# A decoder layer in split fp32 on one core: memory pairs split a block earlier, and DMA turns divided by halves of the tokens

## The chip, the cores and the metric

The kernel runs on one core of one Trainium2 chip. The metric is the device time of one execution in microseconds (us). The engines appear under short names: PE (TensorE, the matmuls; PEld is its loading of weights), ACT (ScalarE), DVE (VectorE), POOL (GpSimd) and SP (SyncE, which here issues nearly all DMAs; SPq in the profile is its DMA queue). L399 is line 399 of the kernel. A "half-word" is one of the two 16-bit halves of a 4-byte float.

## The reference

One decoder layer on 256 tokens of width 2048 with 256 memory tokens, all in float32:

```python
hn = rmsnorm(h, norm_mix_w)
q, k, v, g_ret, xr, yr, g_a, g_b = split(hn @ w_in)          # w_in: 2048 x 14336
ret_out = silu(g_ret) * head_groupnorm(retention(rotary(q), rotary(k), v))   # 8 heads
rnn_out = gelu(yr) * rg_lru(causal_dwconv(xr))
merged = sigmoid(g_a) * (ret_out @ w_proj_ret) + sigmoid(g_b) * (rnn_out @ w_proj_rnn)
h = h + merged @ w_mix_out                                   # "mix-out"
h = h + cross_attention(rmsnorm(h), rmsnorm(mem), xa_w_q, xa_w_k, xa_w_v, xa_w_o)  # 4 heads of 512
up = causal_dwconv(rmsnorm(h) @ ffn_w_up)                    # 2048 x 11264
gate, val = split(up)
h = h + (silu(gate) * val) @ ffn_w_down                      # 5632 x 2048
return rmsnorm(h, final_norm_w)
```

The work is in the matrix products with weights; each weight is read once.

## The kernel before

**Products.** Every float32 operand is split into a high part that the matmul's format holds exactly (fp32r) and the low rest, and a product is three matmuls: high by high, high by low and low by high. The weights lie in one array in the order in which they are used. A "chunk" is four tiles of 128 rows by 512 columns (1 MB). SP loads it into one of three `raw` buffers (L252); ACT copies each half of it into `hi` (L279, the cast) and DVE subtracts to get `lo` (L280). Two chunks are prepared ahead (`AHEAD`), and three chunks' worth of `hi` and `lo` are held. A chunk is 24 matmuls with 512 columns (L214). One product with 2048 rows of weights and 512 columns (a "block") is four chunks.

**Order.** PE's matmuls keep the order in which the program states them (`mm`, L213). On the other engines, SP among them, a scheduler orders the instructions; `tc.high_priority` lets what stands in it go ahead of other ready work. Work that follows a block isn't stated at once but by `later(n, fn)` (L286): `fn` is called n + 1 chunks on, so that PE has other matmuls in front of those that need its result. The same queue carries the splits, sums of squares and softmax steps.

**Turns.** A product's result has tokens on the partitions, while the next product wants features there. `by_dma` (L380) turns 256 tokens by 512 features: ACT copies the float rows into `planes` (`pl`), which holds for each half of the tokens (`tt`, 128 tokens) all low half-words and then all high ones (L388, two copies of 1024 elements per partition); SP issues two DMA transposes, one for each half of the tokens, into `turned_` (`pt`, L390); and `later(wait, join)` has ACT put the half-words together again in `f` (L399, two copies, each writing every second half-word). There are 59 turns, so 118 plane copies, 118 transposes and 118 join copies. Callers: `turned_rows` (L404: DVE first scales or copies the two halves of the rows, L412) for the rotary inputs, the convolutions' inputs, keys and queries, and the up blocks of the FFN; `two_heads` in the retention (scaling on ACT, L666); the gated merge; `residual` (L843, the sum with the residual rows `nat` is L855); and the softmax. What follows a join splits its result into the high and low operands `s` of the next products (`split_cols`, L454 on ACT and L455 on DVE, in four steps of 128x256 for a turn's two pairs) or runs the convolutions (L778, L780, L969, L971).

**Memory pairs.** The memory tokens come in already turned. `ms = Pairs(mem_t, p_mem, 3)` (L841) holds eight pairs of 128-feature tiles. `ms.load(n)` issues loads of 256 KB into `xt` (ten buffers, shared with other small tiles); asking for `ms[i]` loads three pairs further and splits pair i with `split_cols`. Pairs 0 to 3 are asked for by `memory_steps` (L877), which `residual` calls at each of the four blocks b of mix-out; the rest by the first key product itself, half-way through each of its chunks. The mix-out blocks run from about 819 to 906 us of the span, the first key block follows, and from 928 us the first query block; the last block of xa_w_o ends near 1290 us, and the first FFN block begins with what its turn yields.

The lines of memory_steps before the change:

```python
        if b == 3:
            ms.load(2)
            for k2 in range(4):
                later(k2, lambda k2=k2: ms[k2])
```

Of the kernel before, what the change touches and what calls it, by code (L numbers as in the profile page):

```python
# [12 lines left out]
U16 = mybir.dt.uint16  # L13
# [4 lines left out]
P = 128  # L18
# [18 lines left out]
FREE = 300  # L37
# [101 lines left out]
def hybrid_layer(  # L139
# [16 lines left out]
    act, dve, pe, pool, sp = nc.scalar, nc.vector, nc.tensor, nc.gpsimd, nc.sync  # L156
# [15 lines left out]
    def big(shape, dt=F32, s="b"):  # L172
        return bp.tile(shape, dt, tag="big", name=nm(s))
# [114 lines left out]
    def later(n, fn):  # L288

        pending.append((step[0] + n + 1, fn))  # L290
# [89 lines left out]
    def by_dma(rows, then, wait=1):  # L380


        planes = big([P, 2, 2, BW], U16, s="pl")
        turned_ = big([P, 2, 4, S], U16, s="pt")
        words = rows.bitcast(U16).rearrange("p t (n h) -> p h t n", h=2)
        with tc.high_priority(FREE):
            for h in range(2):
                act.copy(planes[:, :, h, :], words[:, h])  # L388
        for tt in range(2):
            sp.dma_start_transpose(  # L390
                out=turned_.rearrange("p h f s -> p (h f) s")[:, :, tt * P : (tt + 1) * P],
                in_=planes[:, tt].rearrange("p h n -> p (h n)"),
            )

        def join():
            f = big([P, 4, S], s="f")
            halves_ = f.bitcast(U16).rearrange("p f (s h) -> p h f s", h=2)
            for h in range(2):
                act.copy(halves_[:, h], turned_[:, h])  # L399
            then(f)  # L400

        later(wait, join)

    def turned_rows(a, r, then, wait=1):  # L404

        rows = big([P, 2, BW], s="rows")
        with tc.high_priority(FREE):
            for tt in range(2):
                if r is None:
                    dve.tensor_copy(rows[:, tt, :], a[:, tt, :])  # L410
                else:
                    dve.tensor_scalar_mul(rows[:, tt, :], a[:, tt, :], r[:, tt : tt + 1])  # L412
        by_dma(rows, then, wait)
# [78 lines left out]
    def sum_squares(rows, ss, c, pin=False):  # L492

        for tt in range(2):
            junk = tp.tile([P, BW], F32, tag="tmp", name=nm("junk"))
            i = act.activation(junk, rows[:, tt, :], AF.Square, accum_out=ss[:, tt, c : c + 1])
            if pin:
                tc.keep_in_program_order(i)

    def sums():  # L500
        return sp_.tile([P, 2, 4], F32, tag="ss0", name=nm("ss"))

    def rstd_rows(ss):

        var = sp_.tile([P, 2], F32, tag="var", name=nm("var"))
        dve.tensor_reduce(out=var, in_=ss, axis=AX.X, op=ALU.add)
        return rsqrt_small(var, 2, 1.0 / D, EPS)
# [97 lines left out]
    ret, words = [], []  # L605
# [5 lines left out]
    def retain(g, qr, kr, vs, dec, gates):  # L611
# [36 lines left out]
        def normalise():  # L648
            rstd = rsqrt_small(stats[:, :, 1], 8, 1.0, GN_EPS).rearrange("p (h t) -> p h t", t=2)
            for tt in range(2):  # L650
                dve.tensor_scalar_mul(rstd[:, :, tt], rstd[:, :, tt], rs0[:, tt : tt + 1])
            for hh in range(4):
                for tt in range(2):
                    y = raws[hh][:, tt, :]
                    dve.scalar_tensor_tensor(
                        out=y, in0=y, scalar=stats[:, 2 * hh + tt, 0:1],
                        in1=gates[hh // 2][:, tt, (hh % 2) * DV : (hh % 2 + 1) * DV],
                        op0=ALU.subtract, op1=ALU.mult,
                    )

            def two_heads(i):
                rows = big([P, 2, BW], s="rows")
                for hh in (2 * i, 2 * i + 1):
                    for tt in range(2):
                        c = (hh % 2) * DV
                        act.mul(rows[:, tt, c : c + DV], raws[hh][:, tt, :], rstd[:, hh, tt : tt + 1])  # L666
                by_dma(rows, words.append, 4)

            for i in range(2):
                later(i, lambda i=i: two_heads(i))  # L670
# [4 lines left out]
    for g in range(2):  # L675
# [20 lines left out]
        for b in range(2):  # L696
            a = gemm_n("w_in", 0, xs, NT, O_G + g * 1024 + b * BW)
            t = big([P, 2, BW], s="gate")
# [134 lines left out]
    for b in range(4):  # L833
        m = gated(O_GA, "w_proj_ret", ret, b, big([P, 2, BW], s="m"))
        dve.tensor_add(m, m, mb[b])
        by_dma(m, turn_merged, 1 if b < 3 else 3)
# [4 lines left out]
    ms = Pairs(mem_t, p_mem, 3)  # L841
# [35 lines left out]
    def memory_steps(b):  # L877
        if b == 0:
            ss = sums()
            for c in range(4):  # L880
                later(c, lambda c=c: sum_squares(mnat[c], ss, c))
            later(4, lambda: rsms.append(rstd_rows(ss)))
        if b == 3:
            ms.load(2)
            for k2 in range(4):
                later(k2, lambda k2=k2: ms[k2])

    h1s = []
    ss1 = residual("w_mix_out", merged, h1s, p_xa, memory_steps)


# [170 lines left out]
    for kind, b, *n in ff_plan():  # L1062
# [6 lines left out]
        else:  # L1069
            final = b + n[0] == NF // 4  # L1070
            if final:
                wfin = []
                for i in range(2):
                    t = big([P, 2, BW], s="wf")
# [39 lines left out]
```

## Time and profile before

| what | value |
|---|---|
| median of 3 runs | 2010.22 us (2009.7 to 2010.87) |
| profiled execution, its own time | 2008.91 us |
| profiled execution, span from first to last instruction | 2007.1 us |
| mean granted clock of PE | 0.999 of full speed |
| PE busy | 1995.5 us of the span |
| DVE, ACT busy | 1264.2 us, 1248.7 us |
| moved by DMA | 423.02 MB, 211 GB/s on average |

How the views are read. A row of the page's groups has line, engine, operation, output <- input with partitions x elements and type, and the number of instructions; then the busy time of all, the mean duration of one in ns, and the idle time of the engine just before them with what ended most of it. A row of the waits has the waiting engine, operation and line, what it waited for, and then the total in us, the number of times and the longest. A row of the timeline has the start and the busy time in us of a run of like instructions (x4: four of them), and in brackets how long the engine stood before and for what. Rows of DMA issues have the line, the queue, the number, the shortest, median and longest time of the issuing instruction in ns and the times of the first and last one; the row below gives the time from issue to landing. Busy times of PE overlap by its pipeline: a matmul of 0.39 us may follow the last after 0.23.

### The profile page before, as it was taken

How to read it: one execution, taken by the hardware profiler on the slowest of the kernel's cores; microseconds unless marked ns; L12 is line 12 of the kernel's file. 1: busy time of each engine (PE TensorE's matmuls, PEld its weight loads, DVE VectorE, ACT ScalarE, POOL GpSimd, SP SyncE). 2: the span in 40 equal slices, each digit the busy share in tenths (PEclk: the TensorE clock that was granted, in tenths of full speed). 3: DMA queues.
4: the chain of work that ended last, by engine and by line, in shares of the span. 5: the costliest groups of instructions: out<-in, count | busy, mean ns of one | idle time of the engine just before them, and what ended most of it. 6: DMA issues, size and time to landing. Idle time of an engine off the chain costs nothing.

```text
span 2007.1 us, 23602 instructions
## 1 busy us (share of the span) xinstructions
PE 1995.5 (99%) x9044; PEld 1661.7 (83%) x9044; DVE 1264.2 (63%) x1563; ACT 1248.7 (62%) x1506; POOL 7.7 (0%) x12
## 2 busy tenths in 40 slices
PE   9999999999999999999999999999999999999998
PEld 8888888888888888887888888888888888888887
DVE  6857757888545555457555555666775576664675
ACT  6546648888444455577666655767763566744763
POOL 0000000000000000000000000000000000000000
PEclk9999999999999999999999999999999999999999
DMA  8655657665555566787666545666565566655663
GB/s 318 237 209 168 237 201 197 225 203 186 218 197 191 192 209 212 255 255 249 198 221 213 180 170 195 222 197 232 195 226 210 199 196 219 224 209 201 209 231 126
DMA packets 189376, 423.02 MB, mean 211 GB/s; under 512 B 131664, under 2 KB 136400, under 8 KB 144208
## 3 DMA queue, kind: packets, MB, share of 16 engines
q1 hardware_dynamic: 188832, 421.00, 61.9%
q8 instruction: 70, 1.15, 0.2%
q10 hardware_dynamic: 432, 0.53, 0.1%
q14 instruction: 42, 0.34, 0.0%
HBM read 388.46 MB, written 2.10 MB: 195 GB/s over the span
## 4 chain that ended last, share of the span: by engine, by line
PE 97%; DMA 1%; issue 1%; DVE 0%; ACT 0%; SPq 0%; POOLq 0%; POOL 0%; DVEq 0%; ACTq 0%
PE acc L214 95%; PE sm L214 3%; DMA raw<-in_wall 0%; DMA pt<-pl 0%; DVE lo L280 0%; SPq L252 0%; DVE s L455 0%; SPq L533 0%; ACT f L399 0%; ACT nat L1048 0%; ACT junk L873 0%; DVE nat L855 0%; ACT pl L388 0%; ACT hi L279 0%; POOLq L1110 0%
## 5 line engine op out<-in xcount | busy, mean ns | idle before, releaser
L214 PE MATMUL acc<-hi,s 128*128 128x512 f32 (+1 forms) x5680 | 1739.0, 388 | 1.6 <-DVE s L455 1.6
L280 DVE TENSOR_TENSOR lo<-raw,hi 128x1024 fp32r<-128x1024 f32 (+1 forms) x714 | 860.2, 1219 | 645.5 <-ACT hi L279 628.6
L214 PEld LDWEIGHTS acc<-hi,s 128*128 128x128 f32 x5680 | 1061.7, 188 | 218.9 <-DVE s L455 2.4
L214 PE MATMUL acc<-lo,s 128*128 128x512 f32 (+1 forms) x2840 | 1099.8, 387 | 0.0
L279 ACT CAST hi<-raw 128x1024 fp32r<-128x1024 f32 (+1 forms) x712 | 733.7, 1048 | 500.2 <-PE acc L214 433.7
L214 PEld LDWEIGHTS acc<-lo,s 128*128 128x128 f32 x2840 | 533.2, 188 | 109.1
L399 ACT COPY f<-pt 128x1024 uint16<-128x1024 uint16 x118 | 151.5, 1348 | 76.4 <-DMA pt<-pl 76.4
L388 ACT COPY pl<-rows 128x1024 uint16<-128x1024 uint16 x90 | 89.7, 1044 | 63.8 <-DVE rows L412 55.9
L412 DVE TENSOR_SCALAR rows<-acc,ro 128x512 f32<-128x512 f32 x68 | 47.7, 742 | 3.2 <-PE acc L214 3.2
L971 DVE SCALAR_TENSOR_TENSOR fv<-f,pf,fv 128x255 f32<-128x255 f32 (+1 forms) x88 | 35.8, 477 | 0.7 <-ACT fv L969 0.7
L971 DVE SCALAR_TENSOR_TENSOR fg<-f,pf,fg 128x255 f32<-128x255 f32 (+1 forms) x88 | 35.6, 477 | 0.0
L455 DVE SCALAR_TENSOR_TENSOR s<-f,pb,s 128x256 fp32r<-128x256 f32 x48 | 20.1, 479 | 4.7 <-ACT s L454 4.7
L969 ACT ACTIVATE fv<-f,pf 128x256 f32<-128x256 f32 x44 | 22.8, 590 | 0.0
L969 ACT ACTIVATE fg<-f,pf 128x256 f32<-128x256 f32 x44 | 22.8, 591 | 0.0
L431 ACT ACTIVATE s<-fo 128x512 fp32r<-128x512 f32 x22 | 13.6, 633 | 14.2 <-DVE fo L991 14.2
L780 DVE SCALAR_TENSOR_TENSOR xr<-f,pa,xr 128x255 f32<-128x255 f32 (+2 forms) x48 | 19.9, 478 | 3.2 <-ACT xr L778 3.2
L388 ACT COPY pl<-nat 128x1024 uint16<-128x1024 uint16 x16 | 15.9, 1042 | 8.6 <-DVE nat L855 8.6
L454 ACT ACTIVATE s<-f,pb 128x256 fp32r<-128x256 f32 x48 | 20.6, 498 | 0.0
L214 PEld LDWEIGHTS sm<-s,s 128*128 128x128 f32 x144 | 18.8, 191 | 0.9
L214 PE MATMUL sm<-s,s 128*128 128x256 f32 (+1 forms) x144 | 18.6, 279 | 0.0
L214 PE MATMUL acc<-s,hi 128*128 128x512 f32 x64 | 16.5, 394 | 0.6 <-ACT hi L279 0.4
L443 ACT ACTIVATE v<-acc,ro 128x512 fp32r<-128x512 f32 x16 | 10.9, 684 | 7.7 <-DVE v L444 7.7
(152 smaller groups left out, 623.3 us busy)
## 6 DMA issues: line engine op xcount, KB each, us to landing
raw<-in_wall SPq DMA_DIRECT2D x352, 1024.0 KB, 4.9
nat<-in_x SPq DMA_DIRECT2D x8, 512.0 KB, 8.8
raw<-in_wall SPq DMA_DIRECT2D x6, 512.0 KB, 8.3
nat<-in_mem SPq DMA_DIRECT2D x4, 512.0 KB, 9.3
xt<-in_mem_t SPq DMA_DIRECT2D x8, 256.0 KB, 4.6
pt<-pl SPq DMA_TRANSPOSE x118, 4.3
xt<-in_x_t SPq DMA_DIRECT2D x7, 256.0 KB, 8.4
out<-nat SPq DMA_DIRECT2D x6, 256.0 KB, 2.8
```

The lines of the kernel that those rows point to most:

```text
L214: tc.keep_in_program_order(pe.matmul(*a, **k))
L279: act.copy(hi[:, ds], raw[:, cs, :])
L280: dve.tensor_tensor(out=lo[:, ds], in0=raw[:, cs, :], in1=hi[:, ds].bitcast(F32), op=ALU.subtract)
L388: act.copy(planes[:, :, h, :], words[:, h])
L399: act.copy(halves_[:, h], turned_[:, h])
L412: dve.tensor_scalar_mul(rows[:, tt, :], a[:, tt, :], r[:, tt : tt + 1])
L431: act.mul(t[:, :, 0:S], src, scale)
L454: act.activation(t[:, j, 0:S], src[:, j, :], AF.Identity, scale=wcol(j))
L455: dve.scalar_tensor_tensor(out=t[:, j, S:BW], in0=src[:, j, :], scalar=wcol(j), in1=t[:, j, 0:S].bitcast(F32), op0=ALU.mult, op1=ALU.subtract,
L780: dve.scalar_tensor_tensor(out=y[:, s:S], in0=z[:, 0 : S - s], scalar=p_cw(3 - s, t), in1=y[:, s:S], op0=ALU.mult, op1=ALU.add,)
L969: act.activation(y, z[:, j, :], AF.Identity, scale=pf[:, 2, t : t + 1], bias=pf[:, 3, t : t + 1])
L971: dve.scalar_tensor_tensor(out=y[:, s:S], in0=z[:, j, 0 : S - s], scalar=pf[:, 2 - s, t : t + 1], in1=y[:, s:S], op0=ALU.mult, op1=ALU.add,)
```

## The change

It has three parts. In `by_dma` the plane copies are divided by halves of the tokens instead of by halves of the words, and each half's transpose is stated right behind its copy. In `join` the two copies are divided by halves of the tokens too: each takes both half-words of 128 tokens for four tiles of features. In `memory_steps` the four memory pairs are loaded at block 2 of mix-out instead of block 3, and asked for 2 to 5 steps behind its beginning instead of 0 to 3 steps behind that of block 3, which is two chunks sooner.

```diff
@@ by_dma
-        words = rows.bitcast(U16).rearrange("p t (n h) -> p h t n", h=2)
-        with tc.high_priority(FREE):
-            for h in range(2):
-                act.copy(planes[:, :, h, :], words[:, h])
+        words = rows.bitcast(U16).rearrange("p t (n h) -> p t h n", h=2)
         for tt in range(2):
+            with tc.high_priority(FREE):
+                act.copy(planes[:, tt], words[:, tt])
             sp.dma_start_transpose(
                 out=turned_.rearrange("p h f s -> p (h f) s")[:, :, tt * P : (tt + 1) * P],
                 in_=planes[:, tt].rearrange("p h n -> p (h n)"),
@@ join
-            for h in range(2):
-                act.copy(halves_[:, h], turned_[:, h])
+            for tt in range(2):
+                cs = slice(tt * P, (tt + 1) * P)
+                act.copy(halves_[:, :, :, cs], turned_[:, :, :, cs])
             then(f)
@@ memory_steps
-        if b == 3:
+        if b == 2:
             ms.load(2)
             for k2 in range(4):
-                later(k2, lambda k2=k2: ms[k2])
+                later(2 + k2, lambda k2=k2: ms[k2])
```

The numbers of instructions on every engine stay the same, and so does the order on PE and POOL.

## Prediction

> **What bounds the kernel now.** I read the page's first part, then busy time by stretches, then what PE waited for.
>
> ```profile
> span 2007.1 us, 23602 instructions
> PE 1995.5 (99%) x9044; PEld 1661.7 (83%) x9044; DVE 1264.2 (63%) x1563; ACT 1248.7 (62%) x1506; POOL 7.7 (0%) x12
> ...
> L399 ACT COPY f<-pt 128x1024 uint16<-128x1024 uint16 x118 | 151.5, 1348 | 76.4 <-DMA pt<-pl 76.4
> L388 ACT COPY pl<-rows 128x1024 uint16<-128x1024 uint16 x90 | 89.7, 1044 | 63.8 <-DVE rows L412 55.9
> ```
>
> PE is busy for 99% of the span; ACT and DVE, where the change works, for 62% and 63%. The windows view of PE (busy time, count, granted clock, DMA share, GB/s) shows where PE has no gap at all:
>
> ```profile
> 20.00:900.00 880.00, 880.00 (x3960) 1.00 0.62 214
> 925.00:1290.00 365.00, 365.00 (x1702) 1.00 0.62 200
> 1300.00:1985.00 685.00, 685.00 (x3036) 1.00 0.62 209
> ```
>
> 1930.00 us of the three stretches are all busy at the full granted clock: nothing can be won there, only lost. What is left is the head, the tail and two places in between. PE's waits, all of them:
>
> ```profile
> PE acc L214 <- DVE s L455: 1.6, 2, 1.3
> PE warm L211 <- DVE mhalf L206: 1.1, 1, 1.1
> PE acc L214 <- DVE lo L280: 0.5, 2, 0.4
> PE acc L214 <- ACT hi L279: 0.4, 1, 0.4
> PE acc L214 <- DVE hi L277: 0.2, 1, 0.2
> ```
>
> Only the first row is made by what the diff touches: split pairs (L454/L455). The others are the warm-up and the splitting of weights at the two ends. The timeline of PE has the row's two waits, the first at a memory pair, the second at the last block of xa_w_o:
>
> ```profile
> 917.31 0.50 PE L214 MATMUL acc<-hi,s 128*128 128x512 f32 x1
> 919.08 0.50 PE L214 MATMUL acc<-hi,s 128*128 128x512 f32 x1 [1.27 <-DVE s L455]
> ...
> 1295.56 0.39 PE L214 MATMUL acc<-lo,s 128*128 128x512 f32 x1
> 1295.79 0.39 PE L214 MATMUL acc<-hi,s 128*128 128x512 f32 x1
> 1296.55 0.50 PE L214 MATMUL acc<-hi,s 128*128 128x512 f32 x1 [0.37 <-DVE s L455]
> ```
>
> Undisturbed matmuls start 0.23 us apart (1295.56 to 1295.79). From 917.31 to 919.08 are 1.77 us, so 1.54 are lost; 1295.79 to 1296.55 loses 0.53. A smaller loss of the same kind just ahead of 917.31 (0.11, by the same spacing; its rows are left out) makes 2.18 us in all, 0.11% of the time. That is the whole purse.
>
> **Step 1: memory pairs 0 to 3 loaded one block earlier and split two chunk-steps earlier.** It moves four loads of xt on SP, eight ACT and eight DVE instructions; none is added. How the stall comes about, from the timelines of ACT and DVE:
>
> ```profile
> 903.61 1.70 ACT L454 ACTIVATE s<-xt,pb 128x256 fp32r<-128x256 f32 x4
> ...
> 914.86 1.99 ACT L279 CAST hi<-raw 128x1024 fp32r<-128x1024 f32 x2
> 916.75 1.70 ACT L454 ACTIVATE s<-xt,pb 128x256 fp32r<-128x256 f32 x4
> ...
> 910.48 1.21 DVE L855 TENSOR_TENSOR nat<-nat,acc 128x1024 f32<-128x1024 f32 x1
> 918.55 1.67 DVE L455 SCALAR_TENSOR_TENSOR s<-xt,pb,s 128x256 fp32r<-128x256 f32 x4
> ```
>
> The splits of pairs 4 and 5 stand on ACT behind two casts (914.86 + 1.99) and begin at 916.75; DVE's part begins at 918.55 and PE goes on at 919.08. The changed program has these splits ahead of the casts: ACT begins them at 914.86 at the latest, 1.89 us sooner. DVE follows by about one step (1.67 / 4 = 0.42) plus its start, so the first pair is ready near 916.2 and the second near 917.2. PE wants the first at 917.31 + 0.23 = 917.54. The margin is about 1.3 us, against 1.54 missing: **the 917 loss goes, −1.65 with the small one**. Further room: the splits of pairs 0 to 3 (two rows like that at 903.61 on ACT, 3.4 us; two of 1.67 on DVE) leave this stretch for the mix-out block before, so that the sum at 910.48 can be up to 3 us sooner; I don't count it. Late next are the casts, which end 1.70 later than now (918.55 instead of 916.85). Their halves are first used a chunk-step on (24 matmuls x 0.227 = 5.4 us), so PE doesn't see it. The four loads now stand earlier on SP's queue, 256 KB each against a weight load's 1024, 1 MB in all: one weight load's work among 352, brought forward. The casts' waits for weights tell the reserve:
>
> ```profile
> ACT hi L279 <- DMA raw<-in_wall: 20.3, 14, 3.1
> ```
>
> 14 of 712 casts ever waited for a load, and PE at mid-kernel for none. Cost 0; at best also 0, since no wait of PE for a load is there to go, and at worst 3.1, the longest such wait, if the reserve were gone.
>
> **Step 2: planes by halves of the tokens.** Both ways two copies of 128x1024, each reading every second 16-bit half and writing two runs of 512; only which runs changes. Price 1.044 each as now; bounds: 0.85 (two of the 128x256 splits above at 0.425, half as many elements) and the join's 1.348. The first transpose needs only the first copy, and so is issued one copy (1.0 us) sooner; the second keeps its time or loses it to what now stands between. In the changed order, of 59 turns 29 keep their place among the weight loads, in 21 the load that stood ahead of the pair stands between its halves, in 9 behind both. What a load ahead does to a pair, from the SP issues by line (count, duration of the issue, times, and time to landing), first one pair with nothing ahead, then the pair of 1283.7, then the load ahead of that:
>
> ```profile
> L390 SPq DMA_TRANSPOSE pt<-pl x2: 1238/1286/1334, 1028.0 to 1029.3; - x2
> DMA to landing us min/median/max: 3.1/3.2/3.2
> ...
> L390 SPq DMA_TRANSPOSE pt<-pl x2: 1238/2726/4214, 1283.7 to 1285.0; - x2
> DMA to landing us min/median/max: 6.3/6.5/6.7
> ...
> L252 SPq DMA_DIRECT2D raw<-in_wall x1: 327/327/327, 1282.8 to 1282.8; - x1
> DMA to landing us min/median/max: 6.7/6.7/6.7
> ```
>
> With nothing ahead 3.2 us, behind a load 6.5. So the first half gains up to 1.0 + 3.3, the second about nothing.
>
> **Step 3: joins by halves of the tokens.** Each copy still moves 1024 elements, but as eight runs of 128 instead of one of 1024. Nearest row 1.348 (the same copy); bounds 1.044 (a plane copy) and 8 x 0.425 = 3.4, as if each run cost one of the 128x256 instructions above (1.70 / 4). I take 1.35. At the ends 118 copies would be 36 us less or 242 more of ACT's time, which has some 760 idle, 76.4 of it straight ahead of these copies. The first copy can now run while the second half travels.
>
> **The 1296 stall.** Its chain on ACT, and the DVE row that ends it:
>
> ```profile
> 1281.68 2.00 ACT L388 COPY pl<-nat 128x1024 uint16<-128x1024 uint16 x2 [1.18 <-DVE nat L855]
> 1291.38 2.56 ACT L399 COPY f<-pt 128x1024 uint16<-128x1024 uint16 x2 [1.32 <-DMA pt<-pl]
> 1294.75 1.70 ACT L454 ACTIVATE s<-f,pb 128x256 fp32r<-128x256 f32 x4
> ...
> 1296.02 1.67 DVE L455 SCALAR_TENSOR_TENSOR s<-f,pb,s 128x256 fp32r<-128x256 f32 x4
> ```
>
> Here the load falls between the halves. It waits on SP for the first transpose, now issued at 1282.7, whose issue lasts 1.24: the load goes at about 1283.95, 1.14 later than now. The second transpose follows at 1284.3, and lands, behind the load, 6.3 to 6.7 later: 1290.6 to 1291.0, or as late as 1292.4 if the load's delay of 1.14 is passed on whole to the 1291.3 of now. One copy of 1.35 then ends the join at 1292.0 to 1293.8, against 1293.94: gain 0.1 to 1.9, of which 0.53 is wanted. **I take 0.45 of the 0.53.** The delayed load feeds a chunk that PE wants about two chunk-steps of 5.4 us later, so its 1.14 costs 0.
>
> **Elsewhere.** The cover that could go is thinnest where convolutions crowd ACT and DVE:
>
> ```profile
> 313.70 2.56 ACT L399 COPY f<-pt 128x1024 uint16<-128x1024 uint16 x2 [2.62 <-DMA pt<-pl]
> 316.12 1.04 ACT L279 CAST hi<-raw 128x1024 fp32r<-128x1024 f32 x1
> 317.06 2.08 ACT L778 ACTIVATE xr<-f,pa 128x256 f32<-128x256 f32 x4
> ...
> 318.33 4.82 DVE L780 SCALAR_TENSOR_TENSOR xr<-f,pa,xr 128x255 f32<-128x255 f32 x12
> 323.06 1.22 DVE L280 TENSOR_TENSOR lo<-raw,hi 128x1024 fp32r<-128x1024 f32 x1
> ...
> 327.10 0.39 PE L214 MATMUL acc<-lo,s 128*128 128x512 f32 x1
> ```
>
> In the changed order the cast of 316.12 stands behind the convolutions and the copies after them (2.08, 1.70 and 1.99), so it ends about 5.5 later, near 322.6, its subtraction (1.22) near 323.9, for a first use at 327.10: 3.2 us are left of 8.7. So 0 here too, and up to 1.6 us of a loss only at the far end of step 3's price (two copies, 2.0 each above my value, less those 3.2, and about as much again from the next half). **Sum: −1.65 −0.45 = −2.1 us.** The profiled execution's own time is 2008.91, 1.31 under the median of 2010.22; the same difference from the median gives 2008.1.
>
> **A page weighed.** By the issue rows above the half behind a load lands with that load. The Trainium skill, "DMA: Bandwidth & Descriptors", section "Queues, rings and completion order", says that each SDMA engine consumes the descriptors of a ring in order; the trace agrees with its 3.2 us free and 6.5 us behind a load. By it alone splitting the pair around a load would bring the end of a turn nothing, and the sum would be −1.65, not −2.1.
>
> **The rivals.** *Second half no sooner.* The turn ends when the last half lands; if the load between is passed on whole (1292.4 + 1.35 = 1293.8), the 1296 stall stays and only 917 is won: 2010.22 − 1.65 = 2008.6. For it: 21 of 59 turns have a load there. Against: half of the join is already done by then. *Dearer joins.* At 3.4 a copy the last join at 1296 ends 2.05 later than I say, the stall there grows by 0.9 to 1.3, and with 917 won it is 2009.3 to 2009.8. For it: strided output; against: a copy with the same strides takes 1.348, and only the run length changes. *A new small stall* (the 323 stretch, or a moved load) eats the purse: about 2010.0, no change at all. *Slower:* in 30 turns the weight load now waits on SP behind a transpose, which itself waits for its plane copy.
>
> ```profile
> L390 SPq DMA_TRANSPOSE pt<-pl x118: 1232/1321/5372, 77.1 to 1940.3; - x118
> ```
>
> It decides once a load comes later than its reserve, two chunk-steps of 5.4 us less the 1.2 + 1.0 of cast and subtraction: some 8.6. The longest issue seen is 5.37; two such (10.7) pass it by 2.1, and PE loses 2.1 in each such turn. With three of them (6.3 less the 2.1 won) the kernel is measurably slower, with a third of the 21 turns (7) it is 15 − 2 = 13 us later: 2023. Against: in the median an issue takes 1.32, far inside.
>
> **How the numbers follow.** Chances: both stalls go, 2008.1, 0.58 (own range 2007.5 to 2008.9); only 917 goes, 2008.6, 0.15; dearer joins, 2009.6, 0.08; a new small stall, 2010.0, 0.09; the late loads, 2014 to 2023, 0.08; something more than the purse (a sooner head or tail, which no row shows), 0.02. About 0.2% (4.0 us) is what a measurement can tell from no change; the purse of 2.18 is half of that, so a measurable gain is nearly excluded: faster 0.02, same 0.90, slower 0.08. The runs of before spread by 1.2 (2009.7 to 2010.87): the low end is the purse and that spread, 2010.22 − 2.18 − 1.2 = 2006.8, the high end the new small stall and that spread, 2011.2.
>
> **What would show it.** Right: the wait of PE for DVE s falls from 1.6 to under 0.3; ACT's splits of xt near 914 begin ahead of the casts; join copies come one at a time at about 1.35; the three stretches stay all busy. Wrong: join copies above 2; new PE waits for lo or hi in mid-kernel; a wait of hi for raw far above 20.3 in total.

## The result and the profile after

The changed kernel takes 2007.08 us (median of 21 runs, 2006.29 to 2008.04); the kernel before, measured beside it on the same chip, 2009.63 us (21 runs, 2008.25 to 2010.87). The ratio is 0.9986 with a 95% interval of 0.9981 to 0.9992: 2.8 us faster, at least 1.6 and at most 3.8. The profiled execution took 2006.89 us with a span of 2005.0, against 2008.91 and 2007.1.

The page of the changed kernel, its head and the groups of the two kinds of copies (busy time, mean ns of one, idle time before them and its cause):

```profile
span 2005.0 us, 23548 instructions
PE 1994.7 (99%) x9044; PEld 1662.3 (83%) x9044; DVE 1266.3 (63%) x1563; ACT 1255.4 (63%) x1506; POOL 7.7 (0%) x12
...
L399 ACT COPY f<-pt 128x1024 uint16<-128x1024 uint16 x118 | 155.6, 1353 | 91.5 <-DMA pt<-pl 91.5
L388 ACT COPY pl<-rows 128x1024 uint16<-128x1024 uint16 x90 | 89.6, 1043 | 44.7 <-DVE rows L412 40.9
```

All waits of PE in it:

```profile
PE warm L211 <- DVE mhalf L206: 1.1, 1, 1.1
PE acc L214 <- DVE hi L277: 1.0, 1, 1.0
PE acc L214 <- DVE lo L280: 0.4, 2, 0.2
```

The row of 1.6 us for split pairs is gone, and what is left lies in the head and the tail. The windows of PE around the two old stalls, first before, then after (busy time, count, granted clock, DMA share, GB/s):

```profile
900.00:925.00 25.00, 23.73 (x104) 1.00 0.86 295
1290.00:1300.00 10.00, 9.63 (x43) 1.00 0.64 222
```

```profile
900.00:925.00 25.00, 25.00 (x112) 1.00 0.73 216
1290.00:1300.00 10.00, 10.00 (x46) 1.00 0.62 219
```

PE has eight matmuls more in the first stretch and three more in the second. To compare kernels whose clocks are shifted by their heads, I take the starts of the same matmuls, since PE's order is the same in all of them. Counted from the start of the span, matmul 4000 (the first is 0) starts at 889.10 before and at 889.37 after: the head, whose code is the same, came 0.27 later in this execution (and up to 1.3 later in the others below). From there to the 5200th (the mix-out's end and the key block) the kernel before needs 1.79 us more than the changed one, from the 5200th to the 5950th (it holds 1296) 0.67 more, and from there to the end exactly as long. That is 2.46 less in mid-kernel, less 0.27 in the head and 0.02 behind the last matmul: 2.17, the difference of the spans to a hundredth (2007.12 and 2004.96).

All runs below are put in these terms: PE's loss in us against the changed kernel in each stretch. The first column counts from matmul 300, so that the head's shift is left out.

| kernel | before the 4000th | key block (to the 5200th) | 1296 (to the 5950th) | behind | median, us |
|---|---|---|---|---|---|
| before | 0 | 1.79 | 0.67 | 0 | 2009.63 |
| changed | 0 | 0 | 0 | 0 | 2007.08 |
| e1, memory part alone | 0 | 0 | 1.54 | 0 | 2008.5 |
| e10, the same again | 0 | 0 | 1.34 | 0 | one run |
| e2, turns alone | 0 | 1.88 | 0 | 0 | 2009.74 |
| e3, joins undone | 0 | 0 | 2.47 | 4.53 | 2014.33 |
| e4, planes undone | 0 | 0 | 0.05 | 0 | 2007.17 |
| e5, turns, loads further ahead | 0 | 0.06 | 0 | 0 | 2007.59 |
| e6, joins alone | 0 | 6.89 | 0.02 | 0 | 2008.3 |
| e11, the same again | 0 | 0.20 | 0 | 0 | one run |
| e7, e3 with later joins | 0 | 0 | 2.02 | 15.14 | 2023.93 |
| e8, joins twice | 11.42 | 1.14 | 1.49 | 17.23 | 2035.87 |
| e9, memory loads alone | 0 | 0 | 0.93 | 0 | 2008.0 |

The stretches are of one profiled execution each, the medians of 4 to 21 runs on several chips, where the kernel before had medians of 2009.63 to 2010.24. The kernel before also had executions above 2012.5 (7 of 35 beside e1 to e4), but none above 2010.87 beside the changed kernel, so that the changed one had none above 2008.04 doesn't show that they are gone.

### The profile page after: what moved, and what is told of

Same layout as the page of the kernel before. It is cut to its first block, busy times and chain, and to the rows that moved or that the text cites. A ratio compares the mean times of both kernels' runs of the same rounds, so it can differ in the third digit from the quotient of the medians.

```text
span 2005.0 us, 23548 instructions
## 1 busy us (share of the span) xinstructions
PE 1994.7 (99%) x9044; PEld 1662.3 (83%) x9044; DVE 1266.3 (63%) x1563; ACT 1255.4 (63%) x1506; POOL 7.7 (0%) x12
## 4 chain that ended last, share of the span: by engine, by line
PE 98%; DMA 1%; issue 0%; DVE 0%; SPq 0%; ACT 0%; POOLq 0%; POOL 0%; DVEq 0%
PE acc L214 96%; PE sm L214 3%; DMA raw<-in_wall 1%; ACT nat L1048 0%; DVE lo L280 0%; DVE s L455 0%; SPq L252 0%; POOLq L1110 0%; POOL ro L515 0%; DVE junk L1031 0%; SPq L254 0%; DVE nat L1029 0%; SPq L530 0%; DVE rv L513 0%; POOLq L515 0%
## 5 line engine op out<-in xcount | busy, mean ns | idle before, releaser
L399 ACT COPY f<-pt 128x1024 uint16<-128x1024 uint16 x118 | 155.6, 1353 | 91.5 <-DMA pt<-pl 91.5
L989 ACT ACTIVATE ft<-fg 128x512 f32<-128x512 f32 x22 | 13.9, 630 | 7.3 <-DVE fg L971 7.3
```

The lines of the kernel that those rows point to most:

```text
L399: act.copy(halves_[:, :, :, cs], turned_[:, :, :, cs])
L989: act.activation(th, gt[:, cs, :], AF.Tanh, scale=0.5)
```

## The experiments

The first four take the change apart.

**e1: the third part alone.** The kernel before, with

```diff
-        if b == 3:
+        if b == 2:
             ms.load(2)
             for k2 in range(4):
-                later(k2, lambda k2=k2: ms[k2])
+                later(2 + k2, lambda k2=k2: ms[k2])
```

> The kernel before with the third part of the change alone (memory pairs loaded at block 2 and split two chunks sooner). On ACT the splits of pairs 4 and 5 stand behind two casts here, as before. Theory A (step 1 of the prediction: the moved splits are what frees the 917 stall): PE's wait there, 1.54 + 0.11, goes because everything in this stretch runs up to 3 us sooner, and the 1296 wait of about 0.5 stays; 1.6 us under before. Theory B (the 917 stall went because the plane copies by tokens changed the order on ACT, splits ahead of the casts): the wait at 917 stays at 1.0 to 1.6, and the time is within 0.5 of before.

Measured: ratio 0.9986 (0.9978 to 0.9995). The wait at 917 is gone although the splits of pairs 4 and 5 (at 914.82) stand behind two casts (at 912.93); theory A, not B. But the 1296 loss didn't stay at 0.67, it grew to 1.54. PE's timeline of e1, the longer of two waits there:

```profile
1296.94 0.50 PE L214 MATMUL acc<-hi,s 128*128 128x512 f32 x1 [0.75 <-DVE s L455]
```

and the turn ahead of it, on ACT:

```profile
1281.06 2.00 ACT L388 COPY pl<-nat 128x1024 uint16<-128x1024 uint16 x2 [1.06 <-DVE nat L855]
1291.77 2.56 ACT L399 COPY f<-pt 128x1024 uint16<-128x1024 uint16 x2 [2.22 <-DMA pt<-pl]
```

The head of e1 came 1.28 later than that of the kernel before. With that taken out the plane copies start 1.90 sooner than before (1281.68), but the join only 0.89 sooner (1291.38): the transposes took 7.3 to 7.6 us to land instead of 6.3 to 6.7. So 0.87 of the 1.79 won at the key block was waited away here.

**e2: the first two parts alone**, memory pairs at their old place.

> The kernel before with the first two parts (planes and joins by tokens), memory pairs at their old place. On ACT the splits of pairs 4 and 5 stand ahead of the casts here, as in the changed kernel. Theory A: the 917 wait stays at 1 us or more, since the four other pairs still crowd the stretch of 898 to 909; only the 1296 wait goes, 0.5 us under before. Theory B: the splits start 1.9 us sooner by their place alone, the 917 wait is under 0.2, the 1296 wait is gone too, and the time is 2 us under before, that of the changed kernel. If both e1 and e2 lose the 917 wait, each part alone is enough for it.

Measured: ratio 0.9996 (0.9988 to 1.0005), a wait of 1.88 in the key block, none at 1296. Theory A's result; but its place is new. The splits of pairs 4 and 5 do start ahead of the casts, and PE waits nowhere near 917; it waits for pair 6 at 925, whose split waits for its load (timelines of ACT and PE):

```profile
916.81 1.69 ACT L454 ACTIVATE s<-xt,pb 128x256 fp32r<-128x256 f32 x4
918.41 3.88 ACT L279 CAST hi<-raw 128x1024 fp32r<-128x1024 f32 x4
924.48 1.71 ACT L454 ACTIVATE s<-xt,pb 128x256 fp32r<-128x256 f32 x4 [2.19 <-DMA xt<-in_mem_t]
```

```profile
923.38 0.39 PE L214 MATMUL acc<-lo,s 128*128 128x512 f32 x1
925.04 1.02 PE L214 MATMUL acc<-hi,s 128*128 128x512 f32 x2 [1.27 <-ACT s L454]
```

So the better place on ACT does free 917, and moves the wait to the next pair. That points to the loads.

**e3: the joins undone.** The changed kernel, with

```diff
-            for tt in range(2):
-                cs = slice(tt * P, (tt + 1) * P)
-                act.copy(halves_[:, :, :, cs], turned_[:, :, :, cs])
+            for h in range(2):
+                act.copy(halves_[:, h], turned_[:, h])
```

> The changed kernel with the joins by halves of the words again: both join copies wait for the later of the two transposes. If the early first join copy is what frees the 1296 stall, f is ready one copy (1.35, less what the casts fill) later than in the changed kernel, and PE waits 0.5 to 1.0 us there; if the earlier plane copy alone does it, no wait. The 917 wait is gone either way. Time 0.5 to 1.0 over the changed kernel, or equal to it.

Measured: 2014.33, ratio 1.002 (1.0011 to 1.0028): slower than before. The 1296 loss is 2.47, more than the 1.0 expected, and 4.53 are lost in the FFN, of which neither theory knew. The group of the joins in e3 has nearly twice the idle time of before (76.4), and PE waits for subtractions:

```profile
L398 ACT COPY f<-pt 128x1024 uint16<-128x1024 uint16 x118 | 151.7, 1349 | 139.7 <-DMA pt<-pl 139.6
```

```profile
PE acc L214 <- DVE lo L280: 3.9, 4, 2.3
```

The largest of them, in the timelines of SP, ACT and PE of e3:

```profile
1679.04 1.24 SPq L389 DMA_TRANSPOSE pt<-pl  x1
1680.37 0.53 SPq L252 DMA_DIRECT2D raw<-in_wall  x1
1680.99 1.24 SPq L389 DMA_TRANSPOSE pt<-pl  x1
...
1689.11 2.56 ACT L398 COPY f<-pt 128x1024 uint16<-128x1024 uint16 x2 [7.25 <-DMA pt<-pl]
1691.53 1.04 ACT L279 CAST hi<-raw 128x1024 fp32r<-128x1024 f32 x1
...
1699.38 0.50 PE L214 MATMUL acc<-lo,s 128*128 128x512 f32 x1 [2.26 <-DVE lo L280]
```

and the time to landing of its two transposes:

```profile
DMA to landing us min/median/max: 3.4/5.7/8.0
```

The weight load goes between the halves, the second transpose lands behind it, 8.0 us after its issue (3.4 for the first), and ACT stands 7.25 in front of the join with casts behind it. The weights of the cast at 1691.53 had landed at 1681.4 by the trace: it waited for nothing but its place. In the changed kernel, with the same order on SP, ACT does a first join copy and a cast while the second half travels, and no such wait comes about.

**e4: the planes undone.** The changed kernel with

```diff
-        words = rows.bitcast(U16).rearrange("p t (n h) -> p t h n", h=2)
+        words = rows.bitcast(U16).rearrange("p t (n h) -> p h t n", h=2)
+        with tc.high_priority(FREE):
+            for h in range(2):
+                act.copy(planes[:, :, h, :], words[:, h])
         for tt in range(2):
-            with tc.high_priority(FREE):
-                act.copy(planes[:, tt], words[:, tt])
             sp.dma_start_transpose(
```

> The changed kernel with the plane copies by halves of the words again: both transposes start after both copies, behind the weight load as before (issued 1283.7 and 1285.0 in the clock of before, landed 6.3 to 6.7 later, so 1290.4 and 1291.3). The first join copy then runs 1290.4 to 1291.75, the second to 1293.1, against 1293.94 before: 0.84 sooner, more than the 0.53 wanted. If the joins by tokens are what matters: no wait at 1296 (at most 0.2), time equal to the changed kernel. If the earlier first transpose matters: a wait of 0.3 to 0.5 stays.

Measured: 2007.17, ratio 0.9979 (0.997 to 0.9987), 0.05 lost at 1296: level with the changed kernel. The joins by tokens free 1296; the planes by tokens add nothing to them, and with joins by words they cost 5.5 (e3's 7.0 against e1's 1.5; 5.8 by the medians, 2014.33 and 2008.5).

The next runs ask what makes the wait of the key block, a crowd of splits or the loads.

**e5: e2 with the loads further ahead.**

```diff
-    ms = Pairs(mem_t, p_mem, 3)
+    ms = Pairs(mem_t, p_mem, 5)
```

> e2 (planes and joins by tokens, memory splits at their old place) with one number changed: Pairs(mem_t, p_mem, 5), so that the loads of pairs 6 and 7 are issued with those of the other pairs, some 9 us sooner, while no split is moved. In e2 PE lost 1.66 + 0.52 (less 0.23 each) at 925, at pair 6, whose split waited 2.19 for its load. If the late load makes that wait: it is gone, and with it every wait of PE in mid-kernel; 1.8 us under e2 and level with the changed kernel. If the crowd of splits and casts on ACT makes it: the wait at 925 or 918 stays at 1 us or more, and the time is that of e2.

Measured: ratio 0.9978 (0.9965 to 0.999), 0.06 lost in the key block, level with the changed kernel; no split was moved in the program. ACT of e5 at the first memory pair:

```profile
898.92 0.91 ACT L454 ACTIVATE s<-xt,pb 128x256 fp32r<-128x256 f32 x2 [3.77 <-DMA xt<-in_mem_t]
```

It waits for that pair longer than in the kernel before (2.08), and the splits of pairs 4 and 5 begin at 916.14, which with the heads' shift taken out is 0.3 later than in e2; what differs is that pairs 6 and 7 have landed. So the late load of pair 6 was the wait of e2, and a late first pair cost PE nothing here, where the splits stand ahead of the casts and no later load is waited for.

**e9: the loads of pairs 0 to 5 at block 2, the splits at their old place**, no turn changed.

```diff
-        if b == 3:
-            ms.load(2)
+        if b == 2:
+            ms.load(6)
             for k2 in range(4):
-                later(k2, lambda k2=k2: ms[k2])
+                later(4 + k2, lambda k2=k2: ms[k2])
```

> The kernel before with all six loads of memory pairs 0 to 5 issued at block 2 of mix-out, in one go, one chunk-step block ahead of the old place; the splits stay where they were, and no turn is changed. On ACT the splits of pairs 4 and 5 stand behind two casts, as before. If the late landing of the bunched loads makes the waits of the key block (before had 3.8 us of waiting for xt on ACT, e6's profile 4.83 for one): the wait at 917 goes, only the 1296 wait of 0.5 to 1.5 stays, and the time is that of e1, 1 to 1.7 under before. If the crowd of splits makes it: 1.5 stays at 917 and the time is within 0.5 of before.

Measured: 2008.0, ratio 0.9991 (0.9982 to 1.0), no loss in the key block, 0.93 at 1296, as e1. The splits of pairs 4 and 5 still stand behind casts (ACT of e9):

```profile
913.60 1.98 ACT L279 CAST hi<-raw 128x1024 fp32r<-128x1024 f32 x2
915.49 1.70 ACT L454 ACTIVATE s<-xt,pb 128x256 fp32r<-128x256 f32 x4
```

So early loads are enough in the order of the kernel before too.

**e6 and e11: the joins by tokens alone**, memory pairs and planes as before (the diff is e3's the other way round, on the kernel before).

> The kernel before with the joins by tokens alone (planes by words, memory pairs at their old place). The joins by tokens free the 1296 wait by themselves (e4 lost it without the planes' part): no wait there, and a wait of 1.3 to 2.2 stays in the key block at 917 to 925. If the planes' part was needed after all without the moved memory pairs: 0.5 stays at 1296 too. Time 0.6 under before, or level with it.

> The kernel of e6 once more, for a profile of a usual execution (e6's own took 2014.06 against a median of 2008.3). If the loads of the memory pairs landing late make e6's long waits: ACT's wait for xt is under 3 us here, PE's wait in the key block 1 to 2.5 us, none at 1296, and no stretch of halved clock.

Measured: 2008.3, ratio 0.9989 (0.9974 to 1.0003, not told from the kernel before); no loss at 1296 to speak of in either execution (0.02 and 0), as expected. In the key block e6's profiled execution (2014.06) lost 6.89, where I had put 1.3 to 2.2, and e11's (2007.23) only 0.20, less than the 1 us I had put as the least. It is one program, and what differs is when the first memory pair lands. The first split on ACT and the residual's sum on DVE some 10 us later, in e11, in the kernel before, and in e6:

```profile
896.63 0.91 ACT L455 ACTIVATE s<-xt,pb 128x256 fp32r<-128x256 f32 x2 [0.92 <-DMA xt<-in_mem_t]
...
909.44 1.21 DVE L856 TENSOR_TENSOR nat<-nat,acc 128x1024 f32<-128x1024 f32 x1
```

```profile
898.60 0.91 ACT L454 ACTIVATE s<-xt,pb 128x256 fp32r<-128x256 f32 x2 [2.08 <-DMA xt<-in_mem_t]
```

```profile
902.02 0.91 ACT L455 ACTIVATE s<-xt,pb 128x256 fp32r<-128x256 f32 x2 [4.83 <-DMA xt<-in_mem_t]
...
914.82 1.21 DVE L856 TENSOR_TENSOR nat<-nat,acc 128x1024 f32<-128x1024 f32 x1
```

With the head's shift taken out (0.55, 0 and 0.70) the first split starts at 896.1, 898.6 and 901.3, the sum at 908.9, 910.5 and 914.1, and PE loses 0.20, 1.79 and 6.89 behind it. In the kernel before all six loads go out together, on SP:

```profile
895.46 3.92 SPq L533 DMA_DIRECT2D xt<-in_mem_t  x6
```

In the changed kernel the first two are issued at 850.79, the next at 864.09 and 874.52, and those of pairs 4 and 5 at 892.00; ACT's splits of pairs 0 to 3 wait for nothing. Its sum is at 907.43:

```profile
850.79 0.90 SPq L533 DMA_DIRECT2D xt<-in_mem_t  x2
```

```profile
907.43 1.21 DVE L855 TENSOR_TENSOR nat<-nat,acc 128x1024 f32<-128x1024 f32 x1
```

**e10: e1 once more**, for its 1296 wait.

> The kernel of e1 once more, for one profile: e1 lost 0.64 + 1.25 (less 0.23 each) at 1296, where before lost 0.76 - 0.23. If that place is bound by the landing of transposes and not by PE's own time, the wait takes what 917 gave in part, and differs between executions by up to 1 us: 0.5 to 1.7 here. If e1's growth was an accident of one execution: 0.5, as before.

Measured: 1.34 lost at 1296 (e1: 1.54). The growth over before's 0.67 is no accident of one execution, and here too the transposes landed late (7.1 to 7.4 us); why they did, with a load ahead of them as before, is not settled.

Two runs on the covers.

**e7: e3 with the joins of the FFN's up blocks one chunk later.**

```diff
-        turned_rows(gemm_n("ffn_w_up", 0, h2s, NT, c0 + b * BW), rs2, turned)
+        turned_rows(gemm_n("ffn_w_up", 0, h2s, NT, c0 + b * BW), rs2, turned, 2)
```

> e3 (planes by tokens, joins by words) with the joins of the FFN's up blocks stated one chunk later (wait 2 instead of 1). e3 lost 1.0, 2.4 and 0.6 us in the FFN to subtractions that stood behind casts that stood behind a waiting join (up to 7.25 us). If the casts queued behind the join are the cause, they are placed ahead of it now, and the three losses go (under 0.5 left); the 1296 loss of e3 (2.3) stays; 4 us under e3. If the weight loads themselves come too late behind the split pairs of transposes, the losses stay at 3 us or more.

Measured: 2023.93, ratio 1.0058 (1.0043 to 1.0073), 10 us over e3 instead of 4 under it. The edit didn't do what I wanted: the casts are still placed behind the waiting join (ACT of e7), and all that follows it is a chunk later too.

```profile
1430.80 1.35 ACT L398 COPY f<-pt 128x1024 uint16<-128x1024 uint16 x1 [5.57 <-DMA pt<-pl]
1432.02 1.99 ACT L279 CAST hi<-raw 128x1024 fp32r<-128x1024 f32 x2
```

The run therefore doesn't tell the two theories of its expectation apart; e3's own rows above (weights landed at 1681.4, cast at 1691.53) speak for the casts behind the join, which is argued from them and not tested. An order with the casts ahead wasn't tried.

**e8: every join copy made twice.**

```diff
-                act.copy(halves_[:, :, :, cs], turned_[:, :, :, cs])
+                for _ in range(2):
+                    act.copy(halves_[:, :, :, cs], turned_[:, :, :, cs])
```

> The changed kernel with every join copy made twice (236 copies of about 1.35 instead of 118, 160 us more on ACT; the price of a join as if the dearer-joins rival of the prediction had come true at 2.7). By the prediction's covers (2 to 11 us elsewhere, 1296 the thinnest with 0.2 to 0.8 left): up to 1.35 to 2.7 us lost at 1296, 0 to 1.6 in the stretch of 303 to 334, nothing in the FFN: 1.5 to 3.5 us over the changed kernel. If covers in the FFN are thinner than read from the trace: 5 us and more.

Measured: 2035.87, ratio 1.0113 (1.008 to 1.0145): 29 us over the changed kernel where I had expected 1.5 to 3.5. The 159 us more on ACT cost PE 31 in the profiled execution: 11.42 before the 4000th matmul, 17.23 in the FFN (some 3 of the 31 come from a halved clock, see the last section). PE's two largest waits:

```profile
PE acc L214 <- DVE lo L280: 14.0, 17, 1.9
PE sm L214 <- ACT pl L388: 3.0, 1, 3.0
```

The covers hold for one copy of 1.35, not for two. The second row is one I hadn't listed: matmuls of the recurrent gates (`sm`). The view names ACT's plane copies, which they don't read; what they read is `xr`, the convolutions' result, which ACT and DVE make just ahead.

No version is shown to beat the changed kernel: e4 and e5 have PE as full between the 4000th matmul and the end, to 0.06, and what remains, head and tail, is touched by none of these edits.

## Why the prediction was right, and where its reasons were not

The forecast was 2.1 us less, 2008.1; measured are 2007.08 (2.55 less than the median beside it, 2.8 by the ratio). The forecast for the profiled execution, 2008.91 − 2.1 = 2006.8, met 2006.89, partly by luck: the mid-kernel gain was 2.46 and the head gave 0.27 back. The median lies inside the range given, but 0.4 under the 2007.5 to 2008.9 of the case that came true: the kernel before had 2009.63 here and not the 2010.22 of three runs from which the forecast was counted. The forecast also took 4.0 us as the least that can be told from no change; with 21 runs of each the interval is 0.0011 wide and leaves 1 out.

- **The purse.** Right in kind: PE was full elsewhere, both stalls went, nothing new came. It was put at 2.18 and was 2.46. I had left out that the matmul behind a resumed one also starts late (0.34 instead of 0.23 behind it, in both places), about 0.1 each, most of the 0.28.
- **Step 1, size right (−1.65; measured 1.79), mechanism wrong.** The size had to come out once the stall went, whatever the cause, so it says nothing for the mechanism. The step said that the splits of pairs 4 and 5 go ahead of two casts and start 1.89 sooner. That move comes from the changed turns, not from the memory part: e1 doesn't have it and loses nothing there; e2 has it, no longer waits at 917, and loses 1.88 at pair 6. The "further room" that I named and did not count, up to 3 us in the stretch before, is what the memory part brings: six bunched loads make ACT wait for the first memory pair, and all behind it is late; e9 removes the wait with these loads alone. e5 cuts the chain at its other end: the first pair is as late as ever, but with the turns' order and pairs 6 and 7 loaded nothing is left for PE to wait for.
- **Step 1, loads.** "Cost 0" was right, though six loads moved and not the four that were counted (asking for `ms[3]` sees to it that six pairs are loaded); casts waited 9.9 us for weights instead of 20.3:

```profile
ACT hi L279 <- DMA raw<-in_wall: 9.9, 9, 3.0
```

- **Step 2.** The first half did come sooner, and it bought nothing: e4 has all of the gain without it. That step 2 without step 3 loses 7.0 us, 5.5 more than with neither (e3 against e1), wasn't seen: the step priced the second half as "about nothing" and did not ask who stands behind the join that waits for it.
- **Step 3, price.** 1.35 forecast, 1.353 measured. Its worth was underrated: a first copy that runs, with a cast behind it, while the second half travels is what frees 1296 and shields the casts.
- **The 1296 stall.** Forecast: load between the halves, join ended 0.1 to 1.9 sooner, 0.45 of 0.53 won. Measured on SP and ACT of the changed kernel:

```profile
1281.12 1.24 SPq L389 DMA_TRANSPOSE pt<-pl  x1
1282.45 0.53 SPq L252 DMA_DIRECT2D raw<-in_wall  x1
1283.07 3.12 SPq L389 DMA_TRANSPOSE pt<-pl  x1
...
1285.07 1.35 ACT L399 COPY f<-pt 128x1024 uint16<-128x1024 uint16 x1
1287.49 1.05 ACT L279 CAST hi<-raw 128x1024 fp32r<-128x1024 f32 x1 [1.07 <-issue]
1290.17 1.35 ACT L399 COPY f<-pt 128x1024 uint16<-128x1024 uint16 x1 [1.62 <-DMA pt<-pl]
```

The join ends at 1290.17 + 1.35 = 1291.52. The plane copies start 1.63 sooner than before (1280.05 against 1281.68), so in the clock of before that is 1293.15 against 1293.94: 0.79 won, all of 0.67 covered. The order was as forecast, the gain inside its range. The second half was not there at 1290.6 to 1291.0, as the step had it, but at about 1291.8 in that clock, later than the 1291.3 of before: the whole gain comes from the one copy that is left to do behind it.
- **The page weighed.** The Trainium skill, "DMA: Bandwidth & Descriptors", section "Queues, rings and completion order", has descriptors consumed in ring order. The second half did land behind the load (about 7 us after its issue here, 8.0 in e3). That the 1296 stall should then stay, the rival built on it, held only where the join waits for both halves at once (e3); with the join in two parts it didn't.
- **Dearer joins.** It didn't happen, and the rival's price was far too low: it counted 1296 alone, 2009.3 to 2009.8 at 3.4 us a copy (its own terms, 2010.22 − 1.65 + 0.9 to 1.3, give 2009.5 to 2009.9), and the stretch of 303 to 334 was put at 1.6 at most; e8 at 2.7 a copy gave 2035.87.
- **Late loads.** No load in the changed kernel came too late for PE (ACT waited 2.44 us for pair 6), and the stretches from 20 to 900, 925 to 1290 and 1300 to 1985 are all busy. The near miss was another one: not the load that waits behind the transpose, but the transpose that lands behind the load (e3).

## What to carry to other kernels

A short stall on a full engine can have its cause some ninety matmuls earlier: before crediting a move with its end, look for the first engine in the chain that waits for a DMA, here ACT for the first of six bunched loads, 20 us ahead of PE's wait. Then look which links the chain needs: it could be cut at its start (e9) or at its end (e5). Where a transfer is issued in halves and other traffic can get between them, let the consumer work in the same halves, or the halving makes it later (2014.3 against 2007.1). Two of the three parts of this change are enough for all of its gain: the memory part and the joins by tokens (e4).

## What the runs showed of the hardware

The granted clock of PE fell to a half in mid-kernel after waits that were each short. In e6 PE was busy for 1.66 of 5 us (waits of 2.87 and 1.78 start to start), and then ran at 0.50 for 3.41 us, its matmuls 0.43 apart instead of 0.23 (windows of PE in e6):

```profile
918.00:921.00 3.00, 1.16 (x6) 1.00 0.98 292
921.00:923.00 2.00, 0.50 (x1) 1.00 1.06 212
...
924.00:925.00 1.00, 1.00 (x4) 0.50 0.96 292
```

e8 has two more such spells of 3.41 us. One follows a wait of 3.39 start to start (386.63 to 390.01), the other a wait of only 2.29 with a busy PE around it (1785.86 to 1788.15; windows of PE in e8):

```profile
1786.00:1788.00 2.00, 0.25 (x2) 1.00 0.00 0
...
1790.00:1791.00 1.00, 1.00 (x4) 0.50 0.97 410
```

Two other waits of 2.29 in e8 (from 1425.71 and 1518.78) and one of 2.65 in e3 (up to 1699.38) left the clock at 1.00, so the length of a wait doesn't decide. The Trainium skill, "TensorE: Matmul & The Clock Gate", section "Why this matters for your kernels", asks for no idle gap of PE over about 3 us; of the three waits or pairs of waits ahead of a fall only that of 3.39 comes near it.

What fits all 13 profiles is a fixed grid. The changes of the granted clock within a run lie whole multiples of 3.413 us apart: the falls of e8, at 389.85, 1789.32 and 2031.66, by 410 and 71 of them, those of e6, at 923.23 and 2008.67, by 318, and the rise at the start and the fall at the end of the changed kernel by 585 (1996.80 us). Counted on this grid, PE stood idle for 1.90, 2.83 and 2.91 us of the 3.41 just ahead of the three falls in mid-kernel, and for at most 1.62 of any step in mid-kernel that kept its clock. These idle times are an estimate, since the ends of matmuls in a profile are modelled. By them one and the same wait costs a spell of half clock or not, as it falls within one step of the grid or across two: the other two waits of 2.29 put 1.45 and 1.41 into a step. e6's 6.89 holds some 1.5 us of slow clock (seven matmuls, each about 0.2 late) beside the waits themselves.

One program can lose 0.2 or 6.9 us at one place. SP issues the six loads of e6 and e11 behind a pair of transposes, in e11 and in e6 (four of e6's six stand in the view's window):

```profile
889.23 4.33 SPq L390 DMA_TRANSPOSE pt<-pl  x2
893.61 2.94 SPq L534 DMA_DIRECT2D xt<-in_mem_t  x6
```

```profile
893.14 4.86 SPq L390 DMA_TRANSPOSE pt<-pl  x2
898.05 2.77 SPq L534 DMA_DIRECT2D xt<-in_mem_t  x4
```

With the heads' shift taken out the loads go out 4.3 us apart and the first lands 5.2 apart (896.1 and 901.3). The pair of transposes, which is late by most of it, follows from the turns of mix-out before it; what makes these late in one execution and not in the other isn't settled.
